# When a small weight is requested: the pooling weights' load moved into the loop over the heads

## The chip, the cores and the metric

The kernel runs on one NeuronCore of a Trainium2 chip. The metric is the device time of one execution in microseconds (us); lower is better. Five engines take part: TensorE (in profile rows PE for matmuls, PEld for its weight loads), VectorE (DVE), ScalarE (ACT), GpSimd (POOL), and SyncE (SP), whose queue requests nearly all loads from memory. Each engine runs its own stream of instructions in order and waits on semaphores for the others.

## The reference

A two-layer encoder over 512 tokens of width 1024, in float32. The change touches the first layer's mixer: differential attention with four heads, beside a pooling mixer of four channel groups. Both outputs are concatenated and go through one output projection.

```python
proj = h @ ab_w_in[e]
q, k, v, u = jnp.split(proj, [DIFF_WIDTH, 2 * DIFF_WIDTH, 3 * DIFF_WIDTH], axis=-1)
a_out = _diff_attention(q, k, v, ab_lambda[e], ab_subln[e], i)
b_out = _pool_mixer(u, pool_w[e], pool_scale[e])
x = x + jnp.concatenate([a_out, b_out], axis=-1) @ ab_w_out[e]
...
# _pool_mixer, for each group g with window w
outs.append((cs - lagged) / count[None, :, None] - ug)
...
y = jnp.einsum('bsgc,gcd->bsgd', r, pool_w) * pool_scale.reshape(POOL_GROUPS, POOL_GROUP_DIM)
```

After the mixer come a feed-forward part, then a second layer with gated linear attention, a second feed-forward part and a norm.

## The kernel before

Activations lie feature by token, in tiles of 128 partitions by 512 tokens. A projection splits weights and activations into a high and a low part (rounded and remainder) and adds three matmuls per block of 128 features (`mm3`, L149 to L151, into a `psmm` bank). The split of a weight is one ScalarE operation (L127) and one VectorE operation (L128).

Most tiles are rows: 54 equal buffers of one tag, `row`. The names `row8`, `row16` and `tmp2` all mean `row`; `tmp` gives a buffer of a tag of its own and a row by turns. In PSUM two tags have four banks each, `mm` and `ax` (in the profile `psmm` and `psax`). Projections use the first; scores, transposes, attention outputs, column sums and the pooling matmul use the second.

The order on each engine is not the program's. A planner takes the instructions of the program with program order as their priority, simulates the engines, and puts an instruction into its engine's stream when its inputs and its buffer are there. The buffers of one tag are handed out in the program order of the instructions that first write them, so a tile can wait for the ones before it in the program even where a buffer is free. `soon()` raises a priority; `issue_after` adds an order. On the chip the streams are then fixed, and each engine runs its own in order.

Big weights come in requests of 1 MB through `load` (L113 to L117). In the first layer they use two buffers in turn, and the request for the next waits until the split of the one before last has read its buffer.

The stage around the change, in program order:

- The loop over the heads (L382 to L394). Turn `h` evicts q and k (`qk_heads`), makes scores and softmax for three groups of query tiles, transposes the softmax of the group before (`transposes`, L354 on TensorE, L356 on ScalarE into the rows `pTs`), and from turn 2 on calls `attend(h - 2)`. Turn 1 also projects the values.
- `attend(h)` (L368 to L379): eight matmuls (L372), square and scaled copy on ScalarE (L375, L377), the column sums (`col_sums`: L203 on ScalarE, L204 on VectorE, the matmuls L205 and L206), `rsqrt` (L217 and L218 on ScalarE, L210 to L212 on VectorE), a multiply (L378) and the split into the two rows of `cat[h]` (L187 on ScalarE, L188 on VectorE).
- The row and the request for the pooling weights, 128 x 512 floats, 256 KB (L396, L397).
- `pooled(i, g)` four times, for the windows 16, 8, 4 and 2: a projection with weights of `wu0`, an eviction (L406), a few shifted adds (L412), a mean less the input (L415 to L418), the pooling matmul with the pooling weights (L420), and the split of its output into `cat[4 + i]` (L181 on ScalarE, L182 on VectorE). Between the first and the second group stand `attend(2)` and the last transposes; behind the fourth `attend(3)`.
- `add_out` (L432 to L448): the output projection with the weights `wo0`. Its first two tiles take the blocks of `cat` in the order 0, 1, 2, 4, 5, 6, 7 and then 3.

Of the kernel before, what the change touches and what calls it, by code (L numbers as in the profile page):

```python
# [35 lines left out]
def trunk(ctx: ExitStack, tc: tile.TileContext, xT, par, lvl, lam4, wqk0, wu0, wv0, poolw, wo0,  # L36
          wgk, wup, wqk1, wv1, wg1, wo1, w1a, w2a, w1b, w2b, gfin, out):
    nc = tc.nc
# [21 lines left out]
    row8 = row16 = tmp2 = row  # L60
# [15 lines left out]
    def tmp(n=S, dt=F32):  # L76
        if not mlp[0] and turn("tmp", 2):
            return row(n, dt)
        return T([P, n], "tmp", 4, dt)

    def PS(tag, shape=(P, S)):
        cnt[0] += 1
        return pp.tile(list(shape), F32, tag=tag, bufs=4, name=f"ps{tag}_{cnt[0]}")
# [101 lines left out]
    def split(src, tiles=None):  # L185
        ah, al = tiles or act_tiles()
        A.activation(ah, src, AF.Copy)  # L187
        V.tensor_tensor(al, src, ah.bitcast(F32), ALU.subtract)  # L188
        return ah, al
# [9 lines left out]
    def col_sums(sq, c):  # L199

        n = sq.shape[-1]
        ps, hi, lo = PS("ax", (P, n)), tmp(n, F32R), tmp(n, F32R)
        ended["sum"] = A.activation(hi, sq, AF.Copy).ins  # L203
        V.scalar_tensor_tensor(out=lo, in0=sq, scalar=c, in1=hi.bitcast(F32), op0=ALU.add, op1=ALU.subtract)  # L204
        PE.matmul(ps, ones_r, hi, start=True, stop=False)  # L205
        PE.matmul(ps, ones_r, lo, start=False, stop=True)  # L206
        return ps
# [7 lines left out]
    def rsqrt(r, v, inv):  # L215

        A.activation(r, v, AF.Ln, scale=inv)  # L217
        A.activation(r, r, AF.Exp, scale=-0.5)  # L218
        return newton(r, v, inv, tmp(r.shape[-1]))
# [49 lines left out]
    for f in range(KB):  # L269
        if f < 2 or f % 2 == 0:  # L270
            c = slice(f * P, (f + (1 if f < 2 else 2)) * P)
# [5 lines left out]
    for kb in range(KB):  # L277
        c = slice(kb * P, (kb + 1) * P)
# [28 lines left out]
    def qk_heads(h):  # L307
        for j in range(2):
            ps = (ps0, ps1)[h][j] if h < 2 else proj_T(st.next(), act)
            t = spare(8 + 2 * (h % 2) + j)  # L310
            with soon():
                V.tensor_tensor(t, ps, rb, ALU.mult)
            qk[h, j] = t

    def scores(h, qts):

        banks = [PS("ax"), PS("ax")]
        res, c0 = [], 0
        for qt in qts:
            n = (qt + 1) * P  # L320
            res.append(([bank[:, c0:c0 + n] for bank in banks], small(2)))
            c0 += n
        for j in range(2):
            pr = slice(64 * j, 64 * j + 64)
            for qt, (views, _) in zip(qts, res):
                PE.matmul(views[j], qk[h, 0][pr, qt * P:(qt + 1) * P], qk[h, 1][pr, :(qt + 1) * P], start=True,  # L326
                          stop=True)
        for views, neg in res:
            n = views[0].shape[-1]
            for j in range(2):  # L330
                V.memset(views[j][0:64, n - 64:n], NEG)
                V.tensor_reduce(out=neg[:, j:j + 1], in_=views[j], op=ALU.max, axis=AX.X)
            V.tensor_scalar(out=neg, in0=neg, scalar1=-0.125, scalar2=None, op0=ALU.mult)
        return res

    def softmax(h, qt, views, neg):

        n = (qt + 1) * P
        es, rs, sums, c2 = [], small(2), small(2), small(1)
        for j in range(2):  # L340
            e = spare(12 + turn("es", 4))
            A.activation(e[:, :n], views[j], AF.Exp, bias=neg[:, j:j + 1], scale=0.125, accum_out=sums[:, j:j + 1])
            es.append(e)
        V.reciprocal(rs, sums)
        V.tensor_tensor(c2, rs[:, 1:2], neglam, ALU.mult)
        V.tensor_scalar(out=es[1][:, :n], in0=es[1][:, :n], scalar1=c2, scalar2=None, op0=ALU.mult)
        V.scalar_tensor_tensor(out=es[0][:, :n], in0=es[0][:, :n], scalar=rs[:, 0:1], in1=es[1][:, :n],
                               op0=ALU.mult, op1=ALU.add)
        return es[0]

    def transposes(h, qt, p):
        pst = PS("ax")
        for kb in range(qt + 1):
            PE.transpose(pst[:, kb * P:(kb + 1) * P], p[:, kb * P:(kb + 1) * P], ident)  # L354
        for kb in range(qt + 1):
            A.activation(pTs[h][kb][:, qt * P:(qt + 1) * P], pst[:, kb * P:(kb + 1) * P], AF.Copy)  # L356
# [3 lines left out]
    def values():  # L360
        r0 = per_token(rb)
        for t, ps in enumerate(proj_tok(Stream(wv0), act)):
            vt = spare(16 + t)
            with soon():
                A.activation(vt, ps, AF.Copy, scale=r0[:, t:t + 1])
            v.append(vt)

    def attend(h):  # L368

        po = PS("ax")  # L370
        for kb in range(NT):
            PE.matmul(po[:, kb * P:], v[kb][:, h * P:(h + 1) * P], pTs[h][kb][:, kb * P:], start=kb == 0,  # L372
                      stop=kb == NT - 1)
        q = tmp()
        A.activation(q, po, AF.Square)  # L375
        o = tmp2()
        A.activation(o, po, AF.Copy, scale=sub8)  # L377
        V.tensor_tensor(o, o, rsqrt(tmp(), col_sums(q, EPS), 1.0 / P), ALU.mult)  # L378
        cat[h] = split(o, (row16(dt=F32R), row16(dt=F32R)))  # L379

    pend = []
    for h in range(NH):  # L382
        qk_heads(h)
        pTs.append([row16() for _ in range(NT)])
        for qts in ((0, 1), (2,), (3,)):
            sc = scores(h, qts)
            for p in pend:
                transposes(*p)
            pend = [(h, qt, softmax(h, qt, *s)) for qt, s in zip(qts, sc)]
        if h == 1:  # L390
            with tc.issue_after(first_sum):
                values()
        if h > 1:
            attend(h - 2)  # L394

    pw = tmp2().rearrange("p (g c) -> p g c", g=4)  # L396
    nc.sync.dma_start(pw, poolw)  # L397
    st = Stream(wu0)

    def pooled(i, g):  # L400
# [596 lines left out]
```

## Time and profile before

| | us |
|---|---|
| median of 3 runs | 1094.1 (1093.93 to 1096.49) |
| the profiled execution | 1094.42 |
| its span, first to last instruction | 1092.6 |
| TensorE busy | 1068.4 |
| VectorE busy | 824.7 |
| ScalarE busy | 540.5 |

Times in rows of the profile count from the span's start. A timeline's row has start, duration, engine, line, operation, what is written and read, shapes and a count; a bracket behind it gives the idle time of that engine ahead of the row and what ended it. A matmul of 512 columns lasts 0.39 us in the rows, but the next starts 0.23 us after it, as matmuls are pipelined.

### The profile page before, as it was taken

What the parts mean: (1) busy time and instruction counts of PE and PEld (TensorE: products, weight loads), DVE (VectorE), ACT (ScalarE), POOL (GpSimd) and SP (SyncE); (2) the same over time, 40 slices, a digit from 0 to 9 for tenths busy, and PEclk for the clock granted to TensorE, in tenths of its full rate; (3) what the DMA queues carried; (4) which work ended last, traced back from release to release, by engine and by line L of the source; (5) the groups of instructions that cost most, each with busy time, mean ns of one, the idle gap of its engine ahead of it and who ended that gap; (6) DMA issues with size and microseconds to landing.
All of it is one profiled execution on the core that took longest, in us unless ns stands there. A gap on an engine that the chain in (4) does not pass through costs nothing.

```text
span 1092.6 us, 12887 instructions
## 1 busy us (share of the span) xinstructions
PE 1068.4 (98%) x4968; PEld 862.5 (79%) x4968; DVE 824.7 (75%) x1234; ACT 540.5 (49%) x894; POOL 2.3 (0%) x20
## 2 busy tenths in 40 slices
PE   7999989999999999999999999999999999999996
PEld 5676658888888888888787778788888888888885
DVE  6757856696597597598869887866696696696696
ACT  6445354455453453454455556854543453443454
POOL 0000000000000000000000000000000000000000
PEclk9999999999999999999999999999999999999999
DMA  6221233305305305203222131332206206206102
GB/s 240 80 81 71 87 116 135 116 1 193 116 1 192 116 1 193 77 17 116 77 77 78 40 117 39 116 139 93 97 1 231 78 3 229 77 4 228 39 0 78
DMA packets 17919, 103.53 MB, mean 95 GB/s; under 512 B 2017, under 2 KB 3041, under 8 KB 6209
## 3 DMA queue, kind: packets, MB, share of 16 engines
q1 hardware_dynamic: 17712, 102.67, 26.2%
q8 instruction: 39, 0.64, 0.2%
q14 instruction: 24, 0.19, 0.0%
q10 hardware_dynamic: 144, 0.03, 0.0%
HBM read 100.59 MB, written 2.10 MB: 94 GB/s over the span
## 4 chain that ended last, share of the span: by engine, by line
PE 89%; ACT 4%; DVE 4%; DMA 1%; issue 1%; SPq 0%; DVEq 0%; ACTq 0%
PE psmm L150 14%; PE psmm L149 14%; PE psmm L151 14%; PE psmm L573 6%; PE psmm L574 6%; PE psmm L575 6%; PE psax L149 3%; PE psax L150 3%; PE psax L151 3%; PE psax L573 2%; PE psax L574 2%; PE psax L575 2%; PE psmm L174 2%; PE psmm L173 2%; PE psmm L175 2%; PE psax L326 1%
## 5 line engine op out<-in xcount | busy, mean ns | idle before, releaser
L127 ACT ACTIVATE wh<-wraw 128x1024 fp32r<-128x1024 f32 x230 | 243.5, 1061 | 392.6 <-PE psmm L150 159.9
L128 DVE TENSOR_TENSOR wl<-wraw,wh 128x1024 fp32r<-128x1024 f32 x230 | 280.6, 1222 | 66.3 <-ACT wh L127 62.7
L149 PE MATMUL psmm<-row,wh 128*128 128x512 f32 x736 | 288.2, 393 | 8.3 <-ACT wh L273 5.6
L150 PE MATMUL psmm<-row,wh 128*128 128x512 f32 x736 | 289.4, 393 | 0.1
L151 PE MATMUL psmm<-row,wl 128*128 128x512 f32 x736 | 288.6, 392 | 0.9 <-DVE wl L128 0.9
L149 PEld LDWEIGHTS psmm<-row,wh 128*128 128x128 f32 x736 | 138.5, 189 | 39.3 <-ACT wh L273 6.4
L151 PEld LDWEIGHTS psmm<-row,wl 128*128 128x128 f32 x736 | 138.6, 188 | 32.1 <-issue 1.8
L150 PEld LDWEIGHTS psmm<-row,wh 128*128 128x128 f32 x736 | 138.6, 188 | 31.1 <-issue 1.8
L573 PE MATMUL psmm<-wh,row 128*128 128x512 f32 x320 | 124.6, 389 | 0.0
L575 PE MATMUL psmm<-wl,row 128*128 128x512 f32 x320 | 124.5, 389 | 0.0
L574 PE MATMUL psmm<-wh,row 128*128 128x512 f32 x320 | 124.5, 389 | 0.0
L548 DVE TENSOR_TENSOR wraw<-wraw 128x1024 f32<-128x1024 f32 x64 | 77.3, 1219 | 0.3
L500 DVE TENSOR_TENSOR row<-row,row 128x512 fp32r<-128x512 f32 x112 | 75.0, 684 | 0.3 <-ACT row L499 0.3
L575 PEld LDWEIGHTS psmm<-wl,row 128*128 128x128 f32 x320 | 60.1, 188 | 12.5
L573 PEld LDWEIGHTS psmm<-wh,row 128*128 128x128 f32 x320 | 60.1, 188 | 12.4
L574 PEld LDWEIGHTS psmm<-wh,row 128*128 128x128 f32 x320 | 60.1, 188 | 12.3
L499 ACT ACTIVATE row<-row 128x512 fp32r<-128x512 f32 x112 | 65.7, 618 | 5.3 <-DVE row L526 5.3
L514 DVE SCALAR_TENSOR_TENSOR tmp<-psmm,rb 128x512 f32<-128x512 f32 x48 | 32.9, 686 | 45.7 <-PE psmm L151 45.7
L519 ACT ACTIVATE row<-tmp 128x256 f32<-128x256 f32 x128 | 45.9, 406 | 11.0 <-DVE tmp L514 10.7
L151 PE MATMUL psax<-row,wl 128*128 128x512 f32 x128 | 49.8, 389 | 0.0
L149 PE MATMUL psax<-row,wh 128*128 128x512 f32 x128 | 49.8, 389 | 0.0
L150 PE MATMUL psax<-row,wh 128*128 128x512 f32 x128 | 49.8, 389 | 0.0
(235 smaller groups left out, 1310.6 us busy)
## 6 DMA issues: line engine op xcount, KB each, us to landing
wraw<-in_w1a SPq DMA_DIRECT2D x16, 1024.0 KB, 4.8
wraw<-in_w2a SPq DMA_DIRECT2D x16, 1024.0 KB, 4.8
wraw<-in_w1b SPq DMA_DIRECT2D x16, 1024.0 KB, 4.8
wraw<-in_w2b SPq DMA_DIRECT2D x16, 1024.0 KB, 4.8
wraw<-in_wo SPq DMA_DIRECT2D x8, 1024.0 KB, 4.7
wraw<-in_wqk SPq DMA_DIRECT2D x7, 1024.0 KB, 4.8
wraw<-in_wv SPq DMA_DIRECT2D x6, 1024.0 KB, 4.8
wraw<-in_wg SPq DMA_DIRECT2D x4, 1024.0 KB, 4.8
```

The source lines that it names most:

```text
L127: ended["hi"] = A.activation(hi, src, AF.Copy).ins
L128: ended["lo"] = V.tensor_tensor(lo, src, hi.bitcast(F32), ALU.subtract).ins
L149: PE.matmul(ps, wh, ah, start=first, stop=False)
L150: PE.matmul(ps, wh, al, start=False, stop=False)
L151: ended["mm"] = PE.matmul(ps, wl, ah, start=False, stop=last).ins
L499: A.activation(hi, src, AF.Copy)
L500: V.tensor_tensor(lo, src, hi.bitcast(F32), ALU.subtract)
L519: A.activation(raw[name][:, j, :], r[:, th * 256:th * 256 + 256], AF.Square)
L548: V.tensor_tensor(out[k], in0[k], in1[k], ALU.subtract)
L573: PE.matmul(ps[t], hi, wh[:, cs], start=f, stop=False, skip_group_check=True)
L574: PE.matmul(ps[t], lo, wh[:, cs], start=False, stop=False, skip_group_check=True)
L575: PE.matmul(ps[t], hi, wl[:, cs], start=False, stop=l, skip_group_check=True)
```

## The change

The two statements move from behind the loop over the heads to the end of its third turn (`h == 2`), behind `attend(0)`. The row is asked for by another of its names.

```diff
         if h > 1:
             attend(h - 2)
-
-    pw = tmp2().rearrange("p (g c) -> p g c", g=4)
-    nc.sync.dma_start(pw, poolw)
+        if h == 2:
+            pw = row8().rearrange("p (g c) -> p g c", g=4)
+            nc.sync.dma_start(pw, poolw)
+
     st = Stream(wu0)
```

## Prediction

> **What bounds the kernel now.** I read the page's totals first, then the windows around the stage the change touches, then SP's timeline, and last TensorE's timeline and its waits in that stage.
>
> ```profile
> span 1092.6 us, 12887 instructions
> PE 1068.4 (98%) x4968; PEld 862.5 (79%) x4968; DVE 824.7 (75%) x1234; ACT 540.5 (49%) x894; POOL 2.3 (0%) x20
> ```
>
> TensorE (PE) is busy 1068.4 of 1092.6 us, so all its idle time together is 24.2 us. An edit can only gain from those 24.2 us, and only where TensorE waits for what the edit moves.
>
> The windows' columns are length, then busy time (and instructions) of PE, PEld, DVE, ACT and POOL, then the granted clock, the DMA share and GB/s.
>
> ```profile
> 119.10:148.40 29.30, 23.44 (x88) 15.03 (x88) 19.24 (x35) 12.74 (x27) 0.56 (x5) 1.00 0.28 99
> 119.10:131.00 11.90, 11.74 (x51) 8.65 (x50) 11.57 (x22) 6.89 (x14) 0.56 (x5) 1.00 0.06 22
> 148.40:158.40 10.00, 10.00 (x43) 7.40 (x41) 5.66 (x9) 4.57 (x9) 0.00 (x0) 1.00 0.48 184
> ```
>
> The stage between the last head and the output projection, 119.1 to 148.4 us, holds 29.30 − 23.44 = 5.86 us of idle TensorE: a quarter of all there is, in 2.7% of the span. Just before its tail (119.1 to 131.0) TensorE is full and so is VectorE (11.57 of 11.90); right after it TensorE is full again. The granted clock is 1.00 throughout, so it is waiting, not throttling.
>
> SP's timeline (start, duration, queue, line, operation, tile<-tensor) shows where the pooling weights stand:
>
> ```profile
> 53.20 16.16 SPq L116 DMA_DIRECT2D wraw<-in_wu  x2
> 79.97 51.55 SPq L116 DMA_DIRECT2D wraw<-in_wo  x4
> 131.57 0.42 SPq L397 DMA_DIRECT2D row<-in_poolw  x1
> ```
>
> The requests for wo0 one by one, with what it took from issue to landing:
>
> ```profile
> 99.61 0.33 SPq L116 DMA_DIRECT2D wraw<-in_wo  x1
> 115.57 0.33 SPq L116 DMA_DIRECT2D wraw<-in_wo  x1
> 131.19 0.33 SPq L116 DMA_DIRECT2D wraw<-in_wo  x1
> DMA to landing us min/median/max: 4.7/4.8/4.8
> ```
>
> In the code the request of L397 precedes wu0 and wo0. In the queue it comes behind both wu0 requests and all four of wo0, the last of which has just been issued at 131.19. A request that needs nothing but a row was held back by the planner until the second head's rows had been handed out, and then by SP's queue, whose head waited for a weight buffer.
>
> TensorE's timeline of the stage, idle time and its releaser in brackets:
>
> ```profile
> 125.36 0.47 PE L206 MATMUL psax<-tmp,onesr 128*128 128x512 f32 x1
> 131.22 0.50 PE L151 MATMUL psmm<-row,wl 128*128 128x512 f32 x1 [0.34 <-DVE wl L128]
> 132.48 1.20 PE L149 MATMUL psmm<-row,wh 128*128 128x512 f32 x4 [0.76 <-ACT row L187]
> 135.46 0.39 PE L151 MATMUL psmm<-row,wl 128*128 128x512 f32 x1
> 136.59 1.13 PE L420 MATMUL psax<-wraw,row 128*128 128x512 f32 x2 [0.74 <-DMA row<-in_poolw]
> 137.55 2.32 PE L372 MATMUL psax<-row,wraw 128*128 128x512 f32 x8
> 141.65 0.50 PE L205 MATMUL psax<-tmp,onesr 128*128 128x512 f32 x1 [1.78 <-ACT tmp L203]
> 142.00 0.60 PE L354 MATMUL psax<-par,wraw 128*128 128x128 f32 x4
> 142.72 1.88 PE L420 MATMUL psax<-wraw,row 128*128 128x512 f32 x4
> 145.03 1.12 PE L420 MATMUL psax<-wraw,row 128*128 128x512 f32 x2 [0.43 <-DVE tmp L210]
> 147.86 0.74 PE L149 MATMUL psmm<-row,wh 128*128 128x512 f32 x2 [1.71 <-ACT row L187]
> ```
>
> The bracketed gaps add up to 0.34 + 0.76 + 0.74 + 1.78 + 0.43 + 1.71 = 5.76 us. Only 0.74 is put down to the pooling weights. The point to see is the hole in the `psax` work: none between 125.36 and 136.59. Its inputs were there:
>
> ```profile
> 114.24 0.17 DVE L418 TENSOR_TENSOR wraw<-wraw 128x16 f32<-128x16 f32 x1
> 121.23 0.17 DVE L418 TENSOR_TENSOR wraw<-wraw 128x16 f32<-128x16 f32 x1
> 122.03 0.75 DVE L347 SCALAR_TENSOR_TENSOR wraw<-wraw,sm 128x512 f32<-128x512 f32 x1
> 132.99 0.69 DVE L188 TENSOR_TENSOR row<-row,row 128x512 fp32r<-128x512 f32 x1
> ```
>
> Two pooled groups were finished by 121.40 (the first at 114.41), and the last softmax, which L354 at 142.00 transposes, by 122.78. What L372 at 137.55 reads had been ready still earlier. They stood behind L420 of the first group, because the four `psax` banks are handed out in program order, and L420 stood behind the DMA. So the last gaps are one dependent chain, attend(2), started at 137.55 when TensorE had run out of projection work at 135.85.
>
> **The change, part by part.** *Removed* from L397's place: one row, one request (0.42 us on SP). *Added* at the end of turn h = 2: the same. No computing instruction appears or goes, and `tmp`'s alternation is not touched, since both names are plain rows.
>
> *Where the request lands.* Rows are handed out in the order of first writers, so the new place is right behind cat[0]'s pair, whose second row is written at 103.15:
>
> ```profile
> 103.15 0.67 DVE L188 TENSOR_TENSOR row<-row,row 128x512 fp32r<-128x512 f32 x1
> 122.35 1.05 ACT L127 ACTIVATE wh<-wraw 128x1024 fp32r<-128x1024 f32 x1
> L397 SPq DMA_DIRECT2D row<-in_poolw x1: 425/425/425, 131.6 to 131.6; - x1
> DMA to landing us min/median/max: 5.0/5.0/5.0
> ```
>
> That is between wo0's second request (99.61) and its third (115.57). If its row has had no reader before, it needs no wait and goes out at about 100; counting from 103.15 to be safe and adding 5.0 us, it lands by 108.2. The earliest use is after L205/L206 at 125.36, so 17 us are to spare. Cost on SP: 0.42 us ahead of requests that wait until 115.57 and 131.19 for buffers anyway, so nothing. If that cover were gone, it would be 0.42 us once. Should the row have an earlier reader after all, SP would stand for it with wo0's third request behind; that is free as long as the stand ends before 115.57.
>
> *What shares the engines with it.* wo0's second megabyte is in flight then. Its first reader is the ACT split at 122.35, 18 us after it lands (99.61 + 4.8), so a delay of a few microseconds from sharing is free. The 5.0 us of the pooling weights is itself such a shared case: their request followed a megabyte by 0.38 us (131.19 to 131.57).
>
> *What goes.* The wait of 0.74 us, certainly. Then the hole: L420 of the first group can follow L206 at about 125, then attend(2)'s L372 (2.32 us), its L205, and the L354 group, all inside the projections that now fill 125 to 135.
>
> *What is late next.* attend(2) needs rows too, behind those of cat[1] (L188 at 132.99) and of the first pooled split. Its chain's own rows:
>
> ```profile
> 138.47 0.75 DVE L182 SCALAR_TENSOR_TENSOR row<-psax,par,row 128x512 fp32r<-128x512 f32 x1 [4.50 <-ACT row L181]
> 141.63 0.69 DVE L204 SCALAR_TENSOR_TENSOR row<-tmp,tmp 128x512 fp32r<-128x512 f32 x1 [2.41 <-ACT tmp L203]
> 142.38 0.50 PE L206 MATMUL psax<-row,onesr 128*128 128x512 f32 x1
> 158.55 1.17 PE psmm L149 x4
> ```
>
> VectorE, one after the other, from 132.99: 0.69 (L188) + 0.75 (L182) + 0.69 (L204) = 135.12. From L206 on the chain takes what it takes now, 142.38 to 147.86, that is 5.48 us. So cat[2]'s first half stands at about 140.6, where it is 147.86 now. TensorE, with no idle, reaches that use at 147.86 − 5.76 = 142.1: the chain is covered with 1.5 us over. Behind it the same race runs as now. The late matmuls that use cat[3] (the last row, from the chain that ended last) follow cat[2] by 158.55 − 147.86 = 10.7 us, and TensorE works through all of them (10.00 of 10.00 in the window quoted above). As it now starts 1.5 us after cat[2] and not with it, nothing new opens there.
>
> *Sum.* At most 5.76 us. I take off 0.76 for what a reordered stage usually keeps (the size of the gap at 132.48, the kind of stall left where the planner's guess and the chip differ): 5.0 us. Unknown: the stalls that the new order brings. Below they are 0 (gain 5.76); above, the nearest rows are the whole idle time of the present order, 5.76, which would leave nothing. I stand near the lower one, because the chain has slack at both checks. VectorE is the one engine with little room (11.57 of 11.90 until 131), but what moves there, L182 and attend(2)'s four operations, still falls behind 132.99 where it idles (19.24 of 29.30 over the stage).
>
> Downstream TensorE is the bound, so a gain here is kept. The profiled execution took 1094.42 us (span 1092.6 and 1.8 around it), 0.3 above the median of 1094.1. Against its own time the sum is 1094.4 − 5.0 = 1089.4; against the median **1089.1**.
>
> **The rivals.**
>
> *Only the visible wait goes.* If the bubbles behind 137.55 belong to the banks and rows and not to the DMA, the gain is the 0.74 us TensorE waited, or 1.2 counting its weight loader: 1092.9 to 1093.4.
>
> ```profile
> PEld psax L420 <- DMA row<-in_poolw: 1.2, 1, 1.2
> PE psmm L149 <- ACT row L187: 2.5, 2, 1.7
> PE psax L205 <- ACT tmp L203: 1.8, 1, 1.8
> ```
>
> For it: 4.3 of the idle microseconds name ACT, none of them DMA, and the 0.43 before L420 at 145.03 is a bank freed by L210. The Trainium skill, "Perfetto Trace Analysis", section "Optimization Strategy", says that bubbles of one size which repeat can mean too little room for the next tile. By that rule the result is this rival's. The trace speaks mostly against it: the gaps are 0.34 to 1.78 and occur once each. Against the rival stands the hole of 11 us in `psax` with ready inputs.
>
> *Half goes.* cat[1]'s rows gate more than I think, so that attend(2)'s L372 moves only from 137.55 to about 133.7, behind cat[1]'s split (132.99 + 0.69). Everything behind is 3.85 us earlier, less about 1 us for projections that then come in its place: gain 2.0 to 3.9, time 1090.2 to 1092.1.
>
> *Nothing moves.* The planner still puts the request behind wo0's fourth: 1094.1. Against it: its row is handed out 30 us of trace earlier.
>
> *Slower.* The place is attend(2)'s second column-sum matmul, L206. TensorE runs its stream in order. If the planner puts L206 among the projections near 128, while its input (L204) is queued on VectorE behind the pooled groups, TensorE stands until L418 of the last group:
>
> ```profile
> 133.80 0.17 DVE L418 TENSOR_TENSOR wraw<-wraw 128x16 f32<-128x16 f32 x1
> ```
>
> That is 133.80 + 0.17 + 0.7 (L204) − 128 = 6.7 us, and the stand pushes cat[2] and attend(3) as well; with the 2.5 us that L149 waits now for ACT kept, the sum is 9.2 − 5.76: 3.4 us slower, 1097.5. It decides from a stand of 5.76 us on. Against it: the row queue holds L204 behind L188 at 132.99 in the planner's order too.
>
> **How the numbers follow.** About 0.3% (3.3 us) is what a measurement of this kernel can tell from no change. Forecast 1089.1: 0.66. Half: 0.14. Visible wait only: 0.11. Nothing: 0.03. Slower: 0.06. *Faster* than 1090.8: 0.63 of the forecast's 0.66 and 0.05 of the half case, 0.68. *Slower* than 1097.4: 0.04, as the last rival straddles the bound. *Within*: 0.28. Range: low 1087.6, the whole 5.76 us plus 0.7 for other orders downstream; high 1093.0, which takes in the half case and the edge of the visible wait and leaves out nothing-moves, slower and most of the visible wait, 0.18 in all.
>
> **What would show it.** The request of `in_poolw` between two wo0 requests near 100 us, and no wait of TensorE on it. L420 first at 125 to 127 and L372 right behind it. cat[2]'s L149 at 142 to 143 with no gap, and idle TensorE over the stage under 1.5 us. The first-layer projections' end and all behind it 5 us earlier, with no other stage changed. Wrong would be: L372 still behind 133; a gap on L206 of several us; or the 5 us won here and lost again after 160.

## The result, and the profile after

| | before | after |
|---|---|---|
| median | 1094.52 us (1093.93 to 1096.49, 4 runs) | 1087.05 us (1086.95 to 1087.28, 4 runs) |
| the profiled execution | 1094.42 us | 1087.09 us |
| its span | 1092.6 us | 1085.3 us |

The ratio is 0.993, with a 95% interval of 0.9918 to 0.9941: 7.5 us faster. The forecast was 1089.1 with a range of 1087.6 to 1093.0, so the direction was right and the gain was half as large again as the 5.0 us forecast, outside the range.

SP's timeline of the changed kernel answers the first question, where the request went. L397 now stands between wo0's second request (the last of the group at 80.01, issued at 99.65) and its third:

```profile
80.01 19.97 SPq L116 DMA_DIRECT2D wraw<-in_wo  x2
100.03 0.43 SPq L397 DMA_DIRECT2D row<-in_poolw  x1
115.64 0.33 SPq L116 DMA_DIRECT2D wraw<-in_wo  x1
```

TensorE's timeline shows the hole of 11 us in the `psax` work filled. L420 of before is L421 here, one line lower:

```profile
124.69 0.43 PE L205 MATMUL psax<-row,onesr 128*128 128x512 f32 x1
124.96 1.02 PE L421 MATMUL psax<-wraw,row 128*128 128x512 f32 x2
125.42 0.80 PE L206 MATMUL psax<-tmp,onesr 128*128 128x512 f32 x1
126.06 2.32 PE L372 MATMUL psax<-row,wraw 128*128 128x512 f32 x8
129.73 0.51 PE L205 MATMUL psax<-tmp,onesr 128*128 128x512 f32 x1
130.07 0.60 PE L354 MATMUL psax<-par,wraw 128*128 128x128 f32 x4
134.14 0.79 PE L206 MATMUL psax<-row,onesr 128*128 128x512 f32 x1
140.00 0.63 PE L149 MATMUL psmm<-row,wh 128*128 128x512 f32 x2
150.42 1.26 PE L149 MATMUL psmm<-row,wh 128*128 128x512 f32 x4
```

The first pooled matmul is at 124.96 instead of 136.59, attend(2) at 126.06 instead of 137.55, cat[2]'s first use at 140.00 instead of 147.86. None of these rows, nor any between them, has a bracket: the profile shows no wait of TensorE in this stage.

The windows compare the stage and what follows. First the kernel before, then the one after (length, then busy time and instructions of PE, PEld, DVE, ACT and POOL, granted clock, DMA share, GB/s). The first window of each runs to the same work: at its end the same instructions come 7.37 us earlier in the kernel after (ScalarE's L127 at 173.01 and at 165.64). The second runs from there to just before the end:

```profile
119.10:170.00 50.90, 45.04 (x179) 31.66 (x179) 35.33 (x57) 26.29 (x47) 0.56 (x5) 1.00 0.32 114
170.00:1092.00 922.00, 912.38 (x4320) 751.75 (x4319) 705.96 (x961) 454.03 (x698) 0.63 (x2) 1.00 0.25 91
```

```profile
119.17:162.63 43.46, 43.42 (x178) 31.92 (x179) 35.89 (x57) 26.15 (x47) 0.56 (x5) 1.00 0.36 126
162.63:1084.63 922.00, 912.43 (x4320) 751.51 (x4319) 705.26 (x961) 454.01 (x698) 0.63 (x2) 1.00 0.26 91
```

The stage shrank by 50.90 − 43.46 = 7.44 us, which is the whole gain; the 922.00 us behind it hold the same work in both. Of the 7.44 us, idle time makes 5.86 − 0.04 = 5.82. The other 45.04 − 43.42 = 1.62 us were counted as *busy* in the kernel before, for the same matmuls. That is the part the prediction did not have.

### The profile page after: what moved, and what is told of

The parts are those of the page before. It is cut to its first block, busy times and chain, and to the rows that moved or that the text cites. A ratio compares the mean times of both kernels' runs of the same rounds, so it can differ in the third digit from the quotient of the medians.

```text
span 1085.3 us, 12887 instructions
## 1 busy us (share of the span) xinstructions
PE 1067.2 (98%) x4968; PEld 863.2 (80%) x4968; DVE 824.7 (76%) x1234; ACT 540.1 (50%) x894; POOL 2.3 (0%) x20
## 4 chain that ended last, share of the span: by engine, by line
PE 91%; ACT 4%; DVE 3%; issue 1%; DMA 1%; SPq 0%; DVEq 0%; ACTq 0%
PE psmm L150 14%; PE psmm L151 14%; PE psmm L149 14%; PE psmm L574 7%; PE psmm L575 7%; PE psmm L576 6%; PE psax L149 3%; PE psax L151 3%; PE psax L150 3%; PE psax L574 3%; PE psax L576 3%; PE psax L575 3%; PE psmm L174 2%; PE psmm L173 2%; PE psmm L175 2%; PE psax L326 1%
## 5 line engine op out<-in xcount | busy, mean ns | idle before, releaser
L127 ACT ACTIVATE wh<-wraw 128x1024 fp32r<-128x1024 f32 x230 | 243.5, 1061 | 392.4 <-PE psmm L150 159.7
L149 PE MATMUL psmm<-row,wh 128*128 128x512 f32 x736 | 288.8, 393 | 5.6 <-ACT wh L273 5.4
L151 PE MATMUL psmm<-row,wl 128*128 128x512 f32 x736 | 289.4, 393 | 0.6 <-DVE wl L128 0.6
L149 PEld LDWEIGHTS psmm<-row,wh 128*128 128x128 f32 x736 | 138.7, 189 | 35.5 <-ACT wh L273 6.2
L151 PEld LDWEIGHTS psmm<-row,wl 128*128 128x128 f32 x736 | 138.8, 189 | 31.8 <-issue 2.3
L151 PE MATMUL psax<-row,wl 128*128 128x512 f32 x128 | 49.8, 389 | 0.0
L149 PE MATMUL psax<-row,wh 128*128 128x512 f32 x128 | 49.8, 389 | 0.0
```

The lines of the kernel that those rows point to most:

```text
L127: ended["hi"] = A.activation(hi, src, AF.Copy).ins
L149: PE.matmul(ps, wh, ah, start=first, stop=False)
L151: ended["mm"] = PE.matmul(ps, wl, ah, start=False, stop=last).ins
```

## The experiments

Two questions: what held the chain back (the order in which rows and banks are handed out, SP's queue, or the late load as such), and where the 1.62 us come from.

**e1_own: the old place, but no row.** The weights go into 512 columns of their own behind the big tile's other parts.

```diff
-    raws = T([P, 24 * S], "wraw", 1)
+    raws = T([P, 24 * S + 48], "wraw", 1)
...
-    pw = tmp2().rearrange("p (g c) -> p g c", g=4)
+    p0 = 20 * S + 3 * (16 + S)
+    pw = raws[:, p0:p0 + S].rearrange("p (g c) -> p g c", g=4)
     nc.sync.dma_start(pw, poolw)
```

> The request stays behind the loop as before, but the weights go into 512 columns of their own at the end of the big tile, outside the rows. Theory (the order in which rows are handed out held the request back; then the psax bank order held everything behind its first reader): the request leaves SP before wo0's, TensorE has no wait in the stage, and the time is that of the changed kernel, 1086.5 to 1087.7. Rival (what helped is the place in the third turn): no gain, 1093.5 to 1095.

Measured: 1087.08 us, ratio 0.9929 (0.9914 to 0.9944). The statement stands where it stood before, behind the loop, and the full gain is there. So the place in the program matters only through the row: without a row to wait for, the planner puts the request ahead of all of wu0's and wo0's, as SP's timeline shows:

```profile
15.82 0.43 SPq L398 DMA_DIRECT2D wraw<-in_poolw  x1
53.16 0.33 SPq L116 DMA_DIRECT2D wraw<-in_wu  x1
```

**e3_act: the old place and the old row, on another queue.**

```diff
-    nc.sync.dma_start(pw, poolw)
+    nc.scalar.dma_start(pw, poolw)
```

> The kernel before, with the request on ScalarE's queue in place of SP's. Theory (row order is the hold): ScalarE comes to it only behind the split of cat[1], at 132 to 133 us; no gain, 1094 to 1096. Rival (SP's queue, whose head waits for a weight buffer, is the hold): the load comes well before 125 us and most of the gain appears, 1087 to 1090.

Measured: 1094.38 us, ratio 0.9993 (0.9984 to 1.0002). ScalarE's timeline shows the request right behind the start of cat[1]'s split, and TensorE's the same gaps as before:

```profile
131.90 0.63 ACT L187 ACTIVATE row<-row 128x512 fp32r<-128x512 f32 x1 [2.59 <-DVE row L378]
131.91 0.34 ACTq L397 DMA_DIRECT2D row<-in_poolw  x1
```

```profile
136.85 1.13 PE L420 MATMUL psax<-wraw,row 128*128 128x512 f32 x2 [0.90 <-DMA row<-in_poolw]
137.81 2.32 PE L372 MATMUL psax<-row,wraw 128*128 128x512 f32 x8
141.91 0.50 PE L205 MATMUL psax<-tmp,onesr 128*128 128x512 f32 x1 [1.78 <-ACT tmp L203]
148.12 0.73 PE L149 MATMUL psmm<-row,wh 128*128 128x512 f32 x2 [1.72 <-ACT row L187]
```

SP's queue, behind whose waiting head the request had stood, was not the hold: off that queue the request comes at 131.91 instead of 131.57, and all six gaps of TensorE are still there. On either queue the request stands beside cat[1]'s split, as it would if its row is handed out only after cat[1]'s.

**e4_late and e5_first: other places for the row.** In e4_late it comes in the fourth turn, right ahead of `attend(1)`; in e5_first ahead of the whole loop.

```diff
+        if h == NH - 1:
+            pw = row8().rearrange("p (g c) -> p g c", g=4)
+            nc.sync.dma_start(pw, poolw)
         if h > 1:
             attend(h - 2)
-        if h == 2:
-            pw = row8().rearrange("p (g c) -> p g c", g=4)
-            nc.sync.dma_start(pw, poolw)
```

> The request in the fourth turn, right ahead of attend(1), so that its row comes just before the rows of cat[1]. Theory: the request leaves SP at about 116 us, behind wo0's third, lands by 121, still ahead of its first use at 125: the same time as the changed kernel, 1086.5 to 1087.7. Rival (earlier is better): part of the gain is lost, 1088.5 or more.

```diff
     pend = []
+    pw = row8().rearrange("p (g c) -> p g c", g=4)
+    nc.sync.dma_start(pw, poolw)
     for h in range(NH):
...
-        if h == 2:
-            pw = row8().rearrange("p (g c) -> p g c", g=4)
-            nc.sync.dma_start(pw, poolw)
```

> The request ahead of the whole loop over the heads. Theory (any place ahead of the rows of cat[1] does, and the stage has no idle TensorE left): the time of the changed kernel, 1086.5 to 1087.7. Rival (a longer lead still gains): 1086.2 or less.

Measured: e4_late 1086.91 us (ratio 0.9928, 0.9913 to 0.9943) and e5_first 1086.96 us (0.9931, 0.9916 to 0.9946). SP's timeline of e4_late:

```profile
115.75 0.42 SPq L395 DMA_DIRECT2D row<-in_poolw  x1
```

The request at 115.75 gains what the one at 100.03 gains, and one ahead of the loop (at 27.74) gains no more. The boundary is where theory has it: `attend(1)`, whose last rows become cat[1]. One call later in the program, and 7.5 us are lost. `attend(1)` writes a few other rows too; which of its rows is the one that holds was not separated.

**e2_swap: the late request kept, the bank order changed.** The kernel before, with attention put ahead of the first pooled group.

```diff
-    pooled(0, 3)
     attend(NH - 2)
     for p in pend:
         transposes(*p)
+    pooled(0, 3)
```

> The kernel before, with attend(2) and the last transposes put ahead of the first pooled group; the request stays where it was. Theory (the loss was not the load's lateness but that attention stood behind its first reader in the bank order): with the load still requested after 125 us, 5.5 to 7.5 us are gained, 1087 to 1089. Rival (the late load itself costs the time): TensorE still waits for it, gain under 2 us, 1092.5 or more.

Measured: 1087.06 us, ratio 0.9927 (0.991 to 0.9943). Its SP and TensorE timelines:

```profile
130.41 0.43 SPq L397 DMA_DIRECT2D row<-in_poolw  x1
```

```profile
125.15 1.02 PE L372 MATMUL psax<-row,wraw 128*128 128x512 f32 x2
129.06 0.50 PE L205 MATMUL psax<-tmp,onesr 128*128 128x512 f32 x1
129.40 0.60 PE L354 MATMUL psax<-par,wraw 128*128 128x128 f32 x4
135.99 2.74 PE L420 MATMUL psax<-wraw,row 128*128 128x512 f32 x6
```

This run carries the explanation. The pooling weights are requested at 130.41, only 1.2 us sooner than in the kernel before, and their first use is at 135.99 against 136.59. The load is as late as ever, and all of the gain is there, because attend(2) no longer stands behind the pooled matmul in program order. The swap puts attend(2)'s rows first as well as its banks, so this run alone does not part the two. But what was late in the kernel before is already attend(2)'s first instruction, L372, and L354 behind it, and these write a `psax` bank and no row: so it is put down to the order of the banks.

**e6_both: the changed kernel with the same swap.** The swap of e2_swap, applied to the kernel after.

> The changed kernel, with attend(2) and the last transposes also put ahead of the first pooled group. Theory (each of the two edits frees the same chain, and what they can win is the same idle time): no further gain, 1086.5 to 1087.7. Rival (two separate gains): 1086 or less.

Measured: 1086.63 us, ratio 0.9929 (0.9912 to 0.9946); the interval overlaps that of the changed kernel. The window of the stage in this run says why nothing was left to win:

```profile
119.10:150.40 31.30, 31.30 (x126) 22.10 (x125) 23.97 (x42) 16.51 (x34) 0.45 (x5) 1.00 0.37 135
```

TensorE is busy for 31.30 of 31.30 us. The fast kernels here, with the request early, attention first, or both, cannot be told apart by these measurements.

**m1_gaps: the price of a gap by itself.** A kernel of matmuls alone, in groups of 12, first without and then with a wait between groups. It was executed once; the granted clock is 1.00 in the part with gaps.

```diff
+    def group(a, n, gap):
+        ps = PS("mm")
+        for i in range(n):
+            PE.matmul(ps, w, a, start=i == 0, stop=i == n - 1)
+        b = row(dt=F32R)
+        A.activation(b, ps, AF.Copy, scale=col)
+        return b if gap else a
...
+    for gap in (False, True):
+        for g in range(NG):
+            a = group(a, 12, gap)
```

> Not the computation: only matmuls of the projections' form (128x512, fp32r). 24 groups of 12 back to back, then 24 groups of 12 in which each group's input is made by ScalarE from the group before, so that TensorE stands once per group. Theory (a gap costs more than the idle time that the profile shows, since the last matmul's row runs on after the next could have started, and the first matmul behind a gap is slow to hand over): time per group with a gap, less time per group without, exceeds the idle time shown per gap by 0.2 to 0.35 us. Rival (the idle time shown is the whole price): by less than 0.05 us.

TensorE's timeline of the part with gaps, two groups one after the other; then, of the changed kernel, two matmuls of a run without gaps that are 12 apart:

```profile
89.59 3.06 PE L275 MATMUL psmm<-row,mw 128*128 128x512 f32 x12 [0.78 <-ACT row L277]
93.42 3.06 PE L275 MATMUL psmm<-row,mw 128*128 128x512 f32 x12 [0.78 <-ACT row L277]
```

```profile
147.02 0.39 PE L149 MATMUL psmm<-row,wh 128*128 128x512 f32 x1
149.74 0.39 PE L149 MATMUL psmm<-row,wh 128*128 128x512 f32 x1
```

Twelve matmuls take 149.74 − 147.02 = 2.72 us from start to start without a gap (in m1_gaps' own part without gaps the pitch is the same 0.227 us from the 13th matmul on), and 93.42 − 89.59 = 3.83 us with one. A gap costs 1.11 us, and the profile shows 0.78 as idle. The other 0.33 us are within the rows counted as busy: the last matmul's row lasts 0.39 us where the next one could have started after 0.23, which is 0.16; the first matmul behind the gap holds the next back for 0.34 us instead of 0.23, which is 0.11; and, by the starts of the single matmuls, the following ten are slower by 0.06 in all.

The kernel before had six bracketed gaps in the stage: 6 × 0.33 = 2.0 us by this price, where the windows show 1.62. The gaps there follow other forms too, and some groups between them are short. The trace of the kernel before also gives the starts of the single matmuls, so each of the six can be priced by itself. Take the wait for the pooling weights: from L151 at 135.46 to L420 at 136.59 are 1.13 us where 0.23 would do, so 0.90 are lost and 0.74 are shown. Behind it the first L420 holds the next back for 0.53 us, where packed ones (these matmuls are slower than the projections') follow each other at 0.43. In the same way the six gaps hide 0.17 to 0.39 us each, 1.65 us together. With the 5.76 us that the brackets show, this is 7.41 us, against 7.44 by which the stage shrank. Other small delays against packed starts come to about 1.3 us in the stage before and after alike.

## Why the prediction was right, and where it was wrong

- *Where the request lands*: right. Forecast between wo0's second and third request at about 100; measured 100.03, with no wait of TensorE on it. Of the two holds that the prediction named in the kernel before, only the order of the rows is borne out; SP's queue as the second is not (e3_act).
- *The hole in the `psax` work*: right. e1_own, e3_act and e4_late show the row order as what held the request. e2_swap shows the program order, and with L372 writing nothing but a bank this is the bank order, as what turned a late load into a late attention.
- *L421 at 125 to 127 and L372 behind it*: right, 124.96 and 126.06.
- *cat[2] no longer last*: right, but by less than forecast. Forecast was its first half at 140.6 and TensorE there at 142.1, so 1.5 us to spare. In the trace the half is ready at 139.80 (L187 below) and L149 uses it at 140.00 without a wait, so 0.20 us to spare. TensorE was there sooner than forecast mostly because 142.1 took the gaps at their bracketed price. The chain was sooner too: VectorE reached L188 of cat[1] at 131.21 instead of 132.99, with the last pooled group's eviction (L407, which was L406 at 129.35) now behind it and not ahead. The prediction had not reckoned with that. First ScalarE's row, then VectorE's, of the kernel after:

```profile
139.17 0.63 ACT L187 ACTIVATE row<-row 128x512 fp32r<-128x512 f32 x1 [2.94 <-DVE row L378]
131.21 0.69 DVE L188 TENSOR_TENSOR row<-row,row 128x512 fp32r<-128x512 f32 x1 [0.70 <-ACT row L187]
132.63 0.68 DVE L407 TENSOR_TENSOR wraw<-psmm,rb 128x512 f32<-128x512 f32 x1
133.22 0.68 DVE L204 SCALAR_TENSOR_TENSOR row<-tmp,tmp 128x512 fp32r<-128x512 f32 x1
```

- *Nothing new opens behind it, and the gain is kept*: right. The stage has 0.04 us of idle TensorE left, and in the rest of the kernel TensorE's busy time is the same to 0.1 us.
- *The sum*: wrong, and here is the step that failed. "At most 5.76 us" took the bracketed idle times as the price of the gaps. The price is the delay from start to start, 0.33 us more for a gap in m1_gaps and 1.65 us more for the six of this stage. Beside that, 0.76 us were taken off for stalls of the new order, and the profile shows 0.04. The terms by measurement: 5.82 idle + 1.62 hidden in busy rows = 7.44, where the prediction had 5.76 − 0.76 = 5.0.
- *The range*: its low end was built on the same bound, "the whole 5.76 us plus 0.7", and so missed by 0.55 us (1087.05 against 1087.6). The text ahead of the prediction even notes that a matmul's row lasts 0.39 us while the next starts 0.23 us after it (true of the projections' matmuls; a row of L420 or a full L372 lasts 0.59, and the next starts 0.43 after it). The sum didn't use it.
- *The rivals*: none came. "Only the visible wait" would have left L372's chain where it was, and its argument, that most of the idle time names ScalarE and not the DMA, misleads: those waits were the exposed chain of a late start. *Half goes* needed L372 behind cat[1]'s split, at 133.7; it stands at 126.06. *Nothing moves* needed the request behind wo0's fourth. The slower case needed L206 ahead of its input; it ran at 134.14 without a wait, but its input (L204 above) had ended only 0.24 us before, at 133.90. The Trainium skill's rule on repeating bubbles ("Perfetto Trace Analysis", section "Optimization Strategy") pointed at too few buffers; in the changed kernel and in e2_swap no buffer was added and the bubbles went, so the order of the four banks was enough to remove them. Whether more banks would have removed them too was not run.

## What to carry to other kernels

Where buffers of one kind are handed out in program order, an instruction that lacks a small input can hold up all later users of that kind: look for a stretch in which an engine has ready work of a kind and issues none, and follow it to the first in line. Cure it by making the first ready sooner, or by putting ready work ahead of it; here either one gave the whole gain, and both together no more. Then check what the freed chain meets: it was covered here by 0.20 us. And price TensorE's gaps from start to start against a packed stretch of the same matmuls, not by the idle time shown.

## What the hardware showed that was not expected

A gap of TensorE costs more than its idle time in the profile: 1.11 us against 0.78 for runs of twelve 128x512 matmuls, because the modelled end of the last one lies 0.16 us beyond where the next could start and the first ones behind the gap are slower (0.34 us, then mostly 0.23 to 0.24, instead of 0.227). Six gaps made the same matmuls of a stage 45.04 us "busy" instead of 43.42.
